# The last 256 tokens of a down projection, turned to have tokens on partitions

## The chip, the core and the metric

The kernel runs on one core of a Trainium2 chip. The core has five engines that run their own instruction streams and wait for each other by semaphores: TensorE (PE, matmuls; its weight loads are listed apart as PEld), VectorE (DVE), ScalarE (ACT), GpSimd (POOL) and SyncE (SP), which here issues most of the DMA transfers. SBUF is the memory on the core, with 128 partitions; PSUM is where matmuls accumulate, in eight banks of 512 fp32 columns. The metric is the device time of one execution in microseconds (us).

## The reference

One layer of an encoder: 2048 tokens, 1024 features. A first RMSNorm and projection, a state-space head group and an attention head group, an output projection; then the part that matters here:

```python
    x = x + mixed @ w_out[l]
    h2 = rmsnorm(x, norm_ffn_g[l])
    x = x + (jax.nn.silu(h2 @ w_gate[l]) * (h2 @ w_up[l])) @ w_down[l]
return rmsnorm(x, norm_final_g)
```

with `rmsnorm(x, g) = x * rsqrt(mean(x * x) + 1e-6) * g`, the mean over the 1024 features of a token. The inner width of the feed-forward part is 2816 = 22 x 128.

## The kernel before, in words

Through the whole kernel activations lie with features on partitions and tokens along the columns. Every matmul in the projections is computed from two fp32r parts of each operand (`split`: a high part by a cast on ACT, a low part by a subtraction on DVE), as three matmuls: high by high, high by low, low by high (`mm3`). fp32r is the reduced fp32 format that the large matmuls use; plain fp32 is used in the small ones: sums against a column of ones, and transposes against the identity.

The phases follow each other: first projection with the set-up of the state-space part (its xt tiles come from a pool of eight buffers), attention and state space, output projection, gate and up projection, down projection. Tile pools give buffers by turn; a scheduler sets the order of each engine's queue, except that PE's instructions keep the order of the program. `high_priority` moves a block ahead in the scheduler's order.

At the start of the gate and up phase SP issues the loads of `lo` (L1370), 20 transfers of 256 KB that bring the transformed activations. The output projection's last two blocks are still running then: they add to `xt` (L1148), store it to DRAM (L1149), square it on ACT (L1154) and load the next `xt` (L1140).

The down projection works in two halves of 1024 tokens. Eight tiles `acc0` to `acc7` (128 features by 1024 tokens each) start as the residual and collect the products. For the second half, 18 of the 22 inner tiles go through `group`; the last four go through `down`, in the token blocks of `TAIL`: 512, 256 and 256 tokens. Per block, `down` takes the eight feature tiles as 4, 2 and 2; per tile it runs 4 x 3 matmuls with the weights of the tile on the array and the block's tokens as moving columns, then DVE adds the bank to `acc` (L1582), and the block's `End` squares the result on ACT and adds up the squares on DVE (L1596 to L1600).

The final norm of a block needs the sum of squares over features, which here is over partitions. `sums` (L1602) multiplies the squares by a column of ones on PE, which gives one value per token, with tokens on partitions; `newton` (L98 to L111) makes the inverse root of it on DVE: 14 small instructions, five to set up and nine for three rounds. `products` (L1607) spreads the values over partitions again by transposes on PE (L79), copies them to SBUF on ACT (L141; the last block reads PSUM), multiplies each `acc` tile by gain and root on DVE (L1612), and stores it (L1613). The sums and products of a block are called between the tile groups of the next one; those of the last block have nothing behind them:

```python
        last.sums(True)
        last.products()
```

Of the kernel before, what the change touches and what calls it, by code (L numbers as in the profile page):

```python
# [16 lines left out]
P = 128  # L17
# [34 lines left out]
ORDER = "sptf"  # L52
PINA = True
X1B = 6
TAIL = (0, 512), (512, 256), (768, 256)
MAGIC = 12582912.0
F2 = NF // 2
SB_, CB_, GB_ = 5, 5, 10
# [52 lines left out]
    return o  # L111


def tok_sums(k, te, ps, c, sq):

    for i in range(4):
        te.matmul(ps[:, c + i : c + i + 1], sq[:, i * P : (i + 1) * P], k.ones[:], start=True, stop=True)


def spread(k, te, pb, o, c):  # L120
# [2 lines left out]
        te.transpose(pb[:, i * P : (i + 1) * P], o[:, c + i : c + i + 1].to_broadcast([P, P]), k.ident[:])  # L123


def rstd_steps(k, te, psum, pool, tag, sq, n, out, nt=None, **kw):

    nt = nt or out.shape[-1] // P
    ps = k.t(psum, *tag, **kw)
    sqs = sq if isinstance(sq, list) else [sq]  # L130
    for i in range(nt):
        for m, sq in enumerate(sqs):
            te.matmul(ps[:, i : i + 1], sq[:, i * P : (i + 1) * P], k.ones[:], start=m == 0, stop=m == len(sqs) - 1)
    with k.tc.high_priority():
        o = newton(k, pool, ps[:, :nt], n, nt)
    yield
    pb = k.t(psum, *tag, **kw)
    for i in range(nt):
        te.transpose(pb[:, i * P : (i + 1) * P], o[:, i : i + 1].to_broadcast([P, P]), k.ident[:])
    if out is not None:  # L140
        k.nc.scalar.copy(out, pb[:, : nt * P])  # L141
    yield pb
# [1371 lines left out]
def down_phase(k, S):  # L1514
    tc, nc, io = k.tc, k.nc, k.io
    V, te = nc.vector, k.te
    with ExitStack() as cx:
# [67 lines left out]
        class End:  # L1585
# [13 lines left out]
                    nc.scalar.activation(t[:, :n], self.acc[i][:, self.ts], AF.Square)  # L1599
                    nc.vector.tensor_tensor(self.sa[m][:, :n], self.sa[m][:, :n], t[:, :n], op=ALU.add)  # L1600

            def sums(self, last=False):  # L1602
                self.rs = None if last else k.t(fa, "rs", [P, 512])
                self.r = rstd_steps(k, k.te, dy, fa, ("ps", [P, 512]), self.sa, D, self.rs[:, : self.n] if self.rs else None, nt=self.n // P)
                next(self.r)

            def products(self):  # L1607
                pb = next(self.r)
                rs = self.rs or pb
                for i, a in enumerate(self.acc):  # L1610
                    v = a[:, self.ts]
                    nc.vector.scalar_tensor_tensor(v, v, k.go[:, i : i + 1], rs[:, : self.n], op0=ALU.mult, op1=ALU.mult)  # L1612
                    nc.sync.dma_start(io["out"][i * P : (i + 1) * P, self.out], a[:, self.ts])  # L1613

        ends = []
        for hf in range(2):
            acc = []
            f0 = 0
            for n, g in enumerate(DGROUPS[hf]):
                group(hf, f0, g, acc, (hf, n) == (0, 0))  # L1620
                f0 += g
                if n in (0, 1):
                    for e in ends:
                        (e.sums, e.products)[n]()
            if hf == 0:
                ends = [End(hf, acc, t, 512) for t in (0, 512)]
                for e in ends:
                    for i in range(KT):
                        e.square(i)
        hs, ds = zip(*((operand(S["h"][m : m + 1]), operand(S["wt"][m : m + 1])) for m in range(4)))  # L1630
        last = None
        for t0, tn in TAIL:
            e = End(1, acc, t0, tn)
            for n, i in enumerate((0, 4, 6)):
                down(hs, ds, range(i, (4, 6, 8)[n]), acc, t0, tn, e)
                if last and n < 2:
                    (last.sums, last.products)[n]()
            last = e
        last.sums(True)
        last.products()  # L1640


def block_kernel(tc, io, phases="pusamf"):
    nc = tc.nc
    k = K(tc, io)
    k.ssm_eng = nc.gpsimd
    with ExitStack() as cx:
        dram = cx.enter_context(tc.tile_pool(name="dram", bufs=1, space=bass.MemoryType.DRAM))
        cp = cx.enter_context(tc.tile_pool(name="const", bufs=1))
# [19 lines left out]
        k.ones = k.t(cp, "ones", [P, 1])  # L1669
        nc.vector.memset(k.ones[:], 1.0)  # L1670
# [12 lines left out]
        with tc.tile_pool(name="mf", reuse_waits="tile", bufs=1) as mf:  # L1683
            with pp() as psum, tc.tile_pool(name="mx", reuse_waits="tile", bufs=1) as mx:
                k.psum, k.mf, k.mx = psum, mf, mx
                for _ in mix:
                    pass
            gate_up_phase(k, S)
            down_phase(k, S)
    return k  # L1690


def layout(inputs):
# [15 lines left out]
    def cg(v):  # L1709
# [9 lines left out]
        "g_mix": cols(a["norm_mix_g"][0]), "g_ffn": cols(a["norm_ffn_g"][0]), "g_final": cols(a["norm_final_g"]),  # L1719
# [27 lines left out]
```

## Time and profile before

| what | us |
|---|---|
| median of 3 runs | 2242.87 (2241.45 to 2247.27) |
| profiled execution | 2241.38 |
| its span, first to last instruction | 2239.6 |
| PE busy in the span | 2153.6 (96%) |
| DVE busy | 1543.1 (69%) |
| ACT busy | 1004.6 (45%) |
| mean granted clock of TensorE | 0.988 |

The span is the part that the trace shows; the execution's own time lies 1.8 us above it. A row of a timeline gives start and duration in us, engine, line, operation, what is written and read, and in brackets how long the engine stood idle before it and what released it. The durations of matmuls contain their way through the array; the distance from start to start is what one costs in a row of them. In groups, the last columns are busy time in us, mean ns of one, and the idle time ahead with its releasers.

### The profile page before, as it was taken

What the parts mean: (1) busy time and instruction counts of PE and PEld (TensorE: products, weight loads), DVE (VectorE), ACT (ScalarE), POOL (GpSimd) and SP (SyncE); (2) the same over time, 40 slices, a digit from 0 to 9 for tenths busy, and PEclk for the clock granted to TensorE, in tenths of its full rate; (3) what the DMA queues carried; (4) which work ended last, traced back from release to release, by engine and by line L of the source; (5) the groups of instructions that cost most, each with busy time, mean ns of one, the idle gap of its engine ahead of it and who ended that gap; (6) DMA issues with size and microseconds to landing.
All of it is one profiled execution on the core that took longest, in us unless ns stands there. A gap on an engine that the chain in (4) does not pass through costs nothing.

```text
span 2239.6 us, 30165 instructions
## 1 busy us (share of the span) xinstructions
PE 2153.6 (96%) x10632; PEld 1819.1 (81%) x10632; DVE 1543.1 (69%) x2706; ACT 1004.6 (45%) x1667; POOL 354.1 (16%) x830
## 2 busy tenths in 40 slices
PE   8988898999988999999999999999999999999997
PEld 6777797999977788788888887888888788888886
DVE  8756767555557666767766768767665577688776
ACT  6355565556567541443333335333333343353322
POOL 3354666666600000000000000000000100000000
PEclk9999999999999999999999999999999999999999
DMA  9778867666552436835645557546333495465642
GB/s 330 231 249 283 270 207 229 193 196 193 179 175 99 137 116 206 275 118 173 198 153 200 198 191 258 199 160 207 108 115 97 136 371 198 159 226 183 217 174 76
DMA packets 194664, 430.16 MB, mean 192 GB/s; under 512 B 19792, under 2 KB 38272, under 8 KB 187408
## 3 DMA queue, kind: packets, MB, share of 16 engines
q1 hardware_dynamic: 186768, 403.26, 54.3%
q0 software_dynamic: 7744, 24.97, 3.6%
q8 instruction: 83, 1.36, 0.3%
q14 instruction: 69, 0.57, 0.1%
HBM read 288.95 MB, written 131.10 MB: 188 GB/s over the span
## 4 chain that ended last, share of the span: by engine, by line
PE 81%; DMA 7%; DVE 6%; ACT 2%; issue 2%; SPq 1%; DVEq 0%; ACTq 0%
PE X L76 20%; PE ps L76 18%; PE pf L76 11%; PE Y L76 10%; PE big L76 7%; PE W L76 5%; PE pj L76 4%; PE pt L79 2%; PE sc L76 2%; DMA acc<-x 1%; DMA hd<-wc 1%; DMA x<-xt 1%; DMA lo<-hc 1%; DMA w<-wss 1%; DVE ptl L900 0%
## 5 line engine op out<-in xcount | busy, mean ns | idle before, releaser
L76 PE MATMUL X<-hi,c 128*128 128x512 f32 x1408 | 450.9, 391 | 6.5 <-DVE c L153 3.4
L76 PE MATMUL ps<-hd,hd 128*128 128x512 f32 (+1 forms) x1968 | 428.1, 379 | 3.3 <-DVE hd L153 2.0
L76 PEld LDWEIGHTS ps<-hd,hd 128*128 128x128 f32 x1968 | 356.4, 188 | 73.6 <-DVE hd L153 2.7
L76 PEld LDWEIGHTS X<-hi,c 128*128 128x128 f32 x1408 | 264.9, 188 | 63.6 <-DVE c L153 4.5
L76 PE MATMUL X<-lo,c 128*128 128x512 f32 x704 | 274.7, 390 | 0.0
L153 ACT CAST hd<-hd 128x1536 fp32r<-128x1536 f32 (+1 forms) x106 | 147.5, 1394 | 231.0 <-DMA hd<-hq 174.6
L76 PE MATMUL Y<-hi,c 128*128 128x512 f32 x704 | 225.2, 390 | 2.4 <-DVE u L1428 2.4
L153 DVE TENSOR_TENSOR hd<-hd 128x1536 fp32r<-128x1536 f32 (+1 forms) x106 | 174.1, 1644 | 38.6 <-ACT hd L153 38.3
L1532 POOL DMA_DIRECT2D hd<-hq x7 | 5.3, 757 | 1165.3 <-PE X L76 1151.2
L153 DVE TENSOR_TENSOR c<-S,c 128x512 fp32r<-128x512 f32 x176 | 120.9, 688 | 99.3 <-ACT c L153 99.0
L1424 ACT COPY u<-X 128x512 f32<-128x512 f32 x132 | 77.5, 588 | 197.4 <-PE X L76 197.3
L153 ACT CAST c<-S 128x512 fp32r<-128x512 f32 x176 | 109.4, 622 | 120.8 <-PE Y L76 61.8
L76 PE MATMUL big<-m,woh 128*128 128x512 f32 x512 | 161.5, 397 | 0.0
L76 PEld LDWEIGHTS Y<-hi,c 128*128 128x128 f32 x704 | 132.6, 188 | 31.0 <-DVE u L1428 3.2
L1566 DVE TENSOR_TENSOR acc<-acc,ps 128x512 f32<-128x512 f32 x196 | 130.1, 682 | 37.9 <-PE ps L76 37.7
L76 PEld LDWEIGHTS X<-lo,c 128*128 128x128 f32 x704 | 132.7, 188 | 27.4
L153 ACT CAST c<-raw 128x512 fp32r<-128x512 f32 x132 | 82.2, 623 | 150.2 <-PE Y L76 73.0
L76 PE MATMUL pf<-hi,w 128*128 128x512 f32 x416 | 148.7, 409 | 0.0
L76 PE MATMUL Y<-lo,c 128*128 128x512 f32 x352 | 137.2, 390 | 0.0
L900 DVE TENSOR_TENSOR ptl<-pt,pth 128x640 fp32r<-128x640 f32 (+3 forms) x152 | 98.3, 647 | 54.6 <-ACT pth L899 53.1
L884 ACT ACTIVATE s<-s,mn 128x640 f32<-128x640 f32 (+4 forms) x128 | 97.9, 765 | 61.9 <-DVE mn L881 58.6
L899 ACT CAST pth<-pt 128x640 fp32r<-128x640 f32 (+3 forms) x152 | 83.7, 551 | 83.2 <-PE pt L79 78.8
(451 smaller groups left out, 4269.1 us busy)
## 6 DMA issues: line engine op xcount, KB each, us to landing
w<-wss SPq DMA_DIRECT2D x36, 1024.0 KB, 6.2
hq<-g SPq DMA_DIRECT2D x140, 256.0 KB, 2.1
hd<-hq SPq DMA_DIRECT2D x35, 768.0 KB, 4.4
hd<-wc SPq DMA_DIRECT2D x35, 768.0 KB, 5.8
raw<-in_w_gate SPq DMA_DIRECT2D x44, 512.0 KB, 3.7
raw<-in_w_up SPq DMA_DIRECT2D x44, 512.0 KB, 4.1
wc<-px SPq DMA_DIRECT2D x66, 256.0 KB, 3.1
wss<-w SPq DMA_DIRECT2D x12, 1024.0 KB, 6.1
```

The lines of the kernel that those rows point to most:

```text
L76: return self.tc.keep_in_program_order(self.tc.nc.tensor.matmul(*a, **b))
L79: return self.tc.keep_in_program_order(self.tc.nc.tensor.transpose(*a, **b))
L153: return nc.scalar.copy(hi, raw), nc.vector.tensor_tensor(lo, raw, f32(hi), op=ALU.subtract)
L884: nc.scalar.activation(s[:, :nk], s[:, :nk], AF.Exp, bias=mn[:], scale=-1.0, accum_out=sums[sb, pr][:, hh, qp : qp + 1])
L899: nc.scalar.copy(pth[:, a:b, qp, :], pt[:, a:b, :])
L900: nc.vector.tensor_tensor(ptl[:, a:b, qp, :], pt[:, a:b, :], f32(pth[:, a:b, qp, :]), op=ALU.subtract)
L1424: nc.scalar.copy(u[:], ps[:])
L1532: (nc.gpsimd if aside else nc.sync).dma_start(f32(lo), src.rearrange("g p c -> p g c"))
L1566: V.tensor_tensor(a, a, ps[:], op=ALU.add)
```

## The change

The `TAIL` keeps the blocks of 512 and of 256 tokens. The last 256 tokens are computed by a new function `by_tokens`, twice, for 128 tokens each, with the operands exchanged: the tokens' activations are the weights on the array, and 512 of the 1024 output features are the moving columns. The result has tokens on partitions. For each of two feature halves (c = 0, 1), 12 matmuls of 512 columns go into one bank, and after the first three of them four plain fp32 matmuls of the `acc` tiles against the identity, which add the residual, transposed, to the bank. The sum of squares is then along a row, and ACT squares and sums a bank in one instruction (`accum_out`). The mean, the root and the root's inverse are values per partition: ACT takes the square root, DVE a reciprocal, and one Newton round corrects it (`refine`). The first half's product with the gain is taken ahead and scaled on ACT; the second half's is one DVE instruction. A block is stored in two transfers of 128 tokens by 512 features, into an output of its own, `out_t`, that is joined to the other on the host.

Since gains now lie along a row, a new input `g_row` is loaded into all 128 partitions, into the tile `rsn`, whose first half is free after the output projection's part. `root`, with the same square root, reciprocal and one round, takes the place of `newton` for the blocks of 512 and 256 tokens of the second half. One square root is called ahead of the tail, so that the table of that function is loaded there.

The core of the diff:

```diff
-TAIL = (0, 512), (512, 256), (768, 256)
+TAIL = (0, 512), (512, 256)
+TOKENS = 768, 896
...
+def root(k, pool, ps, n, w):
+
+    V = k.nc.vector
+    v, f, y, o = (k.t(pool, t, [P, w], bufs=2) for t in ("nv", "nf", "ny", "no"))
+    k.nc.scalar.activation(o[:], ps, AF.Sqrt, scale=1.0 / n, bias=k.eps)
+    V.tensor_scalar(v[:], ps, -0.5 / n, -0.5 * EPS, op0=ALU.mult, op1=ALU.add)
+    return refine(V, v, f, y, o)
+
+def refine(V, v, f, y, o):
+
+    V.reciprocal(y[:], o[:])
+    V.tensor_tensor(f[:], y[:], y[:], op=ALU.mult)
+    V.tensor_tensor(f[:], f[:], v[:], op=ALU.mult)
+    V.scalar_tensor_tensor(o[:], f[:], 1.5, y[:], op0=ALU.add, op1=ALU.mult)
+    return o
...
+        def by_tokens(t0, hs, ds, acc):
+
+            ts = slice(t0, t0 + P)
+            m = (t0 // P) % 2
+            ps = [bank(dx) for _ in range(2)]
+            g, ta = S["rsn"][:, :D], S["rsn"][:, D + m * 512 : D + m * 512 + 512]
+            sq = [k.t(fa, f"q{c}", [P, 1], bufs=2) for c in range(2)]
+            v, f, y, o = (k.t(fa, n, [P, 1], bufs=2) for n in ("nv", "nf", "ny", "no"))
+            for c in range(2):
+                for n, ((hh, hl), (dh, dl)) in enumerate(zip(hs, ds)):
+                    mm3(te, ps[c][:], hh[:, 0, ts], hl[:, 0, ts], dh[:, 0, c * 512 : c * 512 + 512], dl[:, 0, c * 512 : c * 512 + 512], n == 0, n == len(hs) - 1, skip_group_check=True)
+                    if n == 0:
+                        for i in range(4):
+                            te.matmul(ps[c][:, i * P : (i + 1) * P], acc[4 * c + i][:, ts], k.ident[:], start=False, stop=False, skip_group_check=True)
+                    if n % 2:
+                        yield
+                j = k.t(fa, "sg", [P, 512], bufs=2)
+                with tc.high_priority():
+                    nc.scalar.activation(j[:], ps[c][:], AF.Square, accum_out=sq[c][:])
+                    if c == 0:
+                        V.tensor_tensor(ta, ps[0][:], g[:, :512], op=ALU.mult)
+                        V.tensor_scalar(f[:], sq[0][:], 1.0 / D, EPS, op0=ALU.mult, op1=ALU.add)
+                        V.tensor_scalar(y[:], f[:], -0.5, None, op0=ALU.mult)
+            b = k.t(fa, "ob", [P, 512])
+            with tc.high_priority():
+                nc.scalar.activation(o[:], sq[1][:], AF.Sqrt, scale=1.0 / D, bias=f[:])
+                V.tensor_scalar(v[:], sq[1][:], -0.5 / D, y[:], op0=ALU.mult, op1=ALU.add)
+                refine(V, v, f, y, o)
+                nc.scalar.activation(ta, ta, AF.Copy, scale=o[:])
+                V.scalar_tensor_tensor(b[:], ps[1][:], o[:], g[:, 512:], op0=ALU.mult, op1=ALU.mult)
+            rows = slice(t0 - TOKENS[0], t0 - TOKENS[0] + P)
+            nc.sync.dma_start(io["out_t"][rows, :512], ta)
+            nc.sync.dma_start(io["out_t"][rows, 512:], b[:])
+            yield
...
+        nc.sync.dma_start(S["rsn"][:, :D], bass.AP(io["g_row"].tensor, io["g_row"].offset, [[0, P], [1, D]]))
         hs, ds = zip(*((operand(S["h"][m : m + 1]), operand(S["wt"][m : m + 1])) for m in range(4)))
+        nc.scalar.activation(k.t(fa, "q0", [P, 1], bufs=2)[:], k.eps, AF.Sqrt)
         last = None
         for t0, tn in TAIL:
             e = End(1, acc, t0, tn)
             for n, i in enumerate((0, 4, 6)):
                 down(hs, ds, range(i, (4, 6, 8)[n]), acc, t0, tn, e)
-                if last and n < 2:
-                    (last.sums, last.products)[n]()
+                if last and n == 0:
+                    last.sums(root=root)
+                if last and n == 1:
+                    last.products()
             last = e
-        last.sums(True)
-        last.products()
+        for n, _ in enumerate(chain.from_iterable(by_tokens(t0, hs, ds, acc) for t0 in TOKENS)):
+            if n == 2:
+                last.sums(root=root)
+            if n == 5:
+                last.products()
```

What it does to the queues is seen in the order of the built programs. First PE at the very end. `hd` are the split operands, `ps` the PSUM banks, `sa` and `sb` sums of squares, `no` the inverse root. Before, the last two feature tiles of the last block, its sums and its transposes:

```order
L76 MATMUL ps_19990<-hd_19514,hd_19518 128x256 x3
L76 MATMUL ps_19989<-hd_19522,hd_19526 128x256 x3
L76 MATMUL ps_19990<-hd_19522,hd_19526 128x256 x3
L76 MATMUL ps_20023<-ones_85,sa_19898 128x1
L76 MATMUL ps_20023<-ones_85,sb_19901 128x1
...
L79 MATMUL ps_20046<-ident_80,no_20031 128x128 x2
```

Now, from the middle of the second token block's first half (the two transposes are those of the 256 block):

```order
L81 MATMUL ps_19933<-ident_80,no_19889 128x128 x2
L78 MATMUL ps_19915<-hd_19520,hd_19516 128x512 x3
L78 MATMUL ps_19915<-hd_19528,hd_19524 128x512 x3
L78 MATMUL ps_19916<-hd_19504,hd_19500 128x512 x3
L78 MATMUL ps_19916<-ident_80,acc_3276_18347 128x128
L78 MATMUL ps_19916<-ident_80,acc_3277_18348 128x128
L78 MATMUL ps_19916<-ident_80,acc_3278_18349 128x128
L78 MATMUL ps_19916<-ident_80,acc_3279_18350 128x128
L78 MATMUL ps_19916<-hd_19512,hd_19508 128x512 x3
L78 MATMUL ps_19916<-hd_19520,hd_19516 128x512 x3
L78 MATMUL ps_19916<-hd_19528,hd_19524 128x512 x3
```

Nothing of PE is left behind the last projection matmul; the sums and transposes of the 256 block have moved between the matmuls of the token blocks.

Then DVE at the end. Before, the last block's additions and its Newton root, of which the first rows stand here (eight more and eight products follow):

```order
L1582 TENSOR_TENSOR acc_3278_18348<-acc_3278_18348,ps_19989 128x256
L1582 TENSOR_TENSOR acc_3279_18349<-acc_3279_18349,ps_19990 128x256
L1600 TENSOR_TENSOR sb_19901<-sb_19901,sg_20016 128x256
L1600 TENSOR_TENSOR sa_19898<-sa_19898,sg_20020 128x256
L102 TENSOR_SCALAR nv_20028<-ps_20023 128x2
L103 CAST nf_20029<-nv_20028 128x2
L104 TENSOR_SCALAR nf_20029<-nf_20029 128x2
L106 TENSOR_SCALAR nv_20028<-nv_20028 128x2
L105 CAST ny_20030<-nf_20029 128x2
L108 TENSOR_TENSOR nf_20029<-ny_20030 128x2
```

Now, all that follows the fifth product of the 256 block (`q` are the sums of squares of a half, `ob` the second half's result):

```order
L1655 TENSOR_TENSOR rsn_92<-ps_19915,rsn_92 128x512
L1656 TENSOR_SCALAR nf_19920<-q_3435_19917 128x1
L1632 SCALAR_TENSOR_TENSOR acc_3277_18348<-acc_3277_18348,g_final_90,rs_19880 128x256
L1657 TENSOR_SCALAR ny_19921<-nf_19920 128x1
L1632 SCALAR_TENSOR_TENSOR acc_3278_18349<-acc_3278_18349,g_final_90,rs_19880 128x256
L1632 SCALAR_TENSOR_TENSOR acc_3279_18350<-acc_3279_18350,g_final_90,rs_19880 128x256
L1661 TENSOR_SCALAR nv_19919<-q_3436_19918,ny_19921 128x1
L127 RECIPROCAL ny_19921<-no_19922 128x1
L128 TENSOR_TENSOR nf_19920<-ny_19921 128x1
L129 TENSOR_TENSOR nf_19920<-nf_19920,nv_19919 128x1
L130 SCALAR_TENSOR_TENSOR no_19922<-nf_19920,ny_19921 128x1
L1664 SCALAR_TENSOR_TENSOR ob_19982<-ps_19916,no_19922,rsn_92 128x512
```

Behind the last square DVE now has four small steps and one product in place of the root's fourteen and eight products.

Last, SP's queue at the start of the gate and up phase, far from the code's place of the new load. Before, stores of `hc` end and the loads of `lo` begin:

```order
L1323 DMA hc_72<-gh_2036_9941 128x512
L1149 DMA x_5_67<-xt_9846 128x2x512
L1323 DMA hc_72<-gh_2038_9945 128x512
L1323 DMA hc_72<-gl_2037_9943 128x512
L1370 DMA lo_2044_10043<-hc_72 128x512
L1370 DMA lo_2050_10085<-hc_72 128x512
```

Now:

```order
L1343 DMA hc_72<-gh_2036_9942 128x512
L1169 DMA x_5_67<-xt_9847 128x2x512
L1343 DMA hc_72<-gh_2038_9946 128x512
L1343 DMA hc_72<-gl_2037_9944 128x512
L1685 DMA rsn_92<-in_g_row 128x1024
L1390 DMA lo_2044_10044<-hc_72 128x512
L1390 DMA lo_2050_10086<-hc_72 128x512
```

The load of the gains has gone in ahead of the first of the 20 loads; the rows behind it are the same, one place later.

More of the change, by code (lines that the diff above doesn't have):

```diff
@@ L111, in newton @@
     return o
+def root(k, pool, ps, n, w):
[10 more added lines that the diff above has]
+    return o
 def tok_sums(k, te, ps, c, sq):
     for i in range(4):
-        te.matmul(ps[:, c + i : c + i + 1], sq[:, i * P : (i + 1) * P], k.ones[:], start=True, stop=True)
+        te.matmul(ps[:, c + i : c + i + 1], sq[:, i * P : (i + 1) * P], k.ones, start=True, stop=True)
 def spread(k, te, pb, o, c):
@@ L123, in spread, with rstd_steps @@
         te.transpose(pb[:, i * P : (i + 1) * P], o[:, c + i : c + i + 1].to_broadcast([P, P]), k.ident[:])
-def rstd_steps(k, te, psum, pool, tag, sq, n, out, nt=None, **kw):
+def rstd_steps(k, te, psum, pool, tag, sq, n, out, nt=None, root=newton, **kw):
     nt = nt or out.shape[-1] // P
@@ L132, in rstd_steps @@
         for m, sq in enumerate(sqs):
-            te.matmul(ps[:, i : i + 1], sq[:, i * P : (i + 1) * P], k.ones[:], start=m == 0, stop=m == len(sqs) - 1)
+            te.matmul(ps[:, i : i + 1], sq[:, i * P : (i + 1) * P], k.ones, start=m == 0, stop=m == len(sqs) - 1)
     with k.tc.high_priority():
-        o = newton(k, pool, ps[:, :nt], n, nt)
+        o = root(k, pool, ps[:, :nt], n, nt)
     yield
@@ L1600, in square, with sums @@
                     nc.vector.tensor_tensor(self.sa[m][:, :n], self.sa[m][:, :n], t[:, :n], op=ALU.add)
-            def sums(self, last=False):
-                self.rs = None if last else k.t(fa, "rs", [P, 512])
-                self.r = rstd_steps(k, k.te, dy, fa, ("ps", [P, 512]), self.sa, D, self.rs[:, : self.n] if self.rs else None, nt=self.n // P)
+            def sums(self, **kw):
+                self.rs = k.t(fa, "rs", [P, 512])
+                self.r = rstd_steps(k, k.te, dy, fa, ("ps", [P, 512]), self.sa, D, self.rs[:, : self.n], nt=self.n // P, **kw)
                 next(self.r)
             def products(self):
-                pb = next(self.r)
-                rs = self.rs or pb
+                next(self.r)
+                rs = self.rs
                 for i, a in enumerate(self.acc):
@@ L1668, in block_kernel @@
         k.ident = ident
-        k.ones = k.t(cp, "ones", [P, 1])
-        nc.vector.memset(k.ones[:], 1.0)
+        one = k.t(cp, "ones", [P, 2])
+        k.ones, k.eps = one[:, :1], one[:, 1:]
+        nc.vector.memset(k.ones, 1.0)
+        nc.vector.memset(k.eps, EPS)
         k.gm, k.gf, k.go = (k.t(cp, n, [P, KT]) for n in ("g_mix", "g_ffn", "g_final"))
@@ L1741 @@
         io[name] = nc.dram_tensor(f"in_{name}", a.shape, mybir.dt.from_np(a.dtype), kind="ExternalInput").ap()
-    io["out"] = nc.dram_tensor("out", (D, SEQ), F32, kind="ExternalOutput").ap()
+    io["out"] = nc.dram_tensor("out", (D, TOK), F32, kind="ExternalOutput").ap()
+    io["out_t"] = nc.dram_tensor("out_t", (SEQ - TOK, D), F32, kind="ExternalOutput").ap()
     with tile.TileContext(nc) as tc:
@@ L1745 @@
     r = run_bass_kernel_spmd(nc, [arrays], core_ids=[0])
-    return np.ascontiguousarray(r.results[0]["out"].T)[None]
+    return np.ascontiguousarray(np.concatenate([r.results[0]["out"].T, r.results[0]["out_t"]]))[None]
```

3 lines of the change are left out of this document (2 added, 1 removed).

## The prediction

> **What bounds the kernel now.** First the page: its span, and the chain of work that ended last, by engine.
>
> ```profile
> span 2239.6 us, 30165 instructions
> PE 81%; DMA 7%; DVE 6%; ACT 2%; issue 2%; SPq 1%; DVEq 0%; ACTq 0%
> ```
>
> TensorE (PE) is the bound for most of the span, so a change is worth what it takes from the places where PE is not the last to end. The table by stretches, asked around the end of the program (busy us of PE, PEld, DVE, ACT, POOL, then clock and DMA), shows such a place.
>
> ```profile
> 2200.00:2220.00 20.00, 18.79 (x159) 18.58 (x158) 15.18 (x50) 5.22 (x13) 0.00 (x0) 1.00 0.28 106
> 2220.00:2230.00 10.00, 4.99 (x40) 4.50 (x38) 7.74 (x30) 1.94 (x5) 0.00 (x0) 1.00 0.30 106
> 2230.00:2240.00 10.00, 0.66 (x2) 0.29 (x2) 4.45 (x16) 0.00 (x0) 0.00 (x0) 0.50 0.30 106
> ```
>
> In the last 20 us PE works for less than 6. The timeline of PE there (start, duration, what, and in brackets the idle time before and who ended it), then of DVE, and the output line:
>
> ```profile
> 2203.26 3.11 PE L76 MATMUL ps<-hd,hd 128*128 128x256 f32 x24
> 2207.59 0.65 PE L79 MATMUL ps<-ident,no 128*128 128x128 f32 x4 [1.21 <-DVE no L110]
> 2207.99 8.88 PE L76 MATMUL ps<-hd,hd 128*128 128x256 f32 x72
> 2216.71 0.28 PE L76 MATMUL ps<-ones,sa 128*128 128x1 f32 x2
> ...
> 2222.03 0.43 PE L79 MATMUL ps<-ident,no 128*128 128x128 f32 x2 [1.40 <-DVE no L110]
> 2222.21 3.12 PE L76 MATMUL ps<-hd,hd 128*128 128x256 f32 x24
> 2227.85 0.38 PE L76 MATMUL ps<-ones,sa 128*128 128x1 f32 x2 [2.52 <-DVE sa L1600]
> ...
> 2231.62 0.66 PE L79 MATMUL ps<-ident,no 128*128 128x128 f32 x2 [2.72 <-DVE no L110]
> ```
>
> ```profile
> 2232.32 3.22 DVE L1612 SCALAR_TENSOR_TENSOR acc<-acc,g_final,ps 128x256 f32<-128x256 f32 x8 [0.85 <-PE ps L79]
> ```
>
> ```profile
> L1613 SPq DMA_DIRECT2D out<-acc x24: 332/364/537, 2209.7 to 2236.6; - x24
> ```
>
> The last projection matmul ends at 2222.21 + 3.12 = 2225.33; the span runs 14.27 us more. In it a chain passes from engine to engine: additions and squares (to 2227.85), sums over features, the Newton root (2.72 of waiting), the transposes, eight products, stores. The last store is issued at 2236.6 and the span ends 3.0 later.
>
> **The change, part by part: prices.** The change keeps everything up to the first 256-token block, and replaces the second (96 matmuls of 256 columns) by two blocks of 128 tokens with 24 matmuls of 512 columns each, plus 16 matmuls against the identity that bring in the residual. The rows for each kind, PE first:
>
> ```profile
> 2149.77 30.54 PE L76 MATMUL ps<-hd,hd 128*128 128x512 f32 x134
> ```
>
> ```profile
> 2202.45 0.95 PE L76 MATMUL ps<-ones,sa 128*128 128x1 f32 x8
> ```
>
> ```profile
> 337.18 0.59 PE L76 MATMUL pj<-rsn,Tm 128*128 128x256 f32 x2
> 337.61 0.59 PE L76 MATMUL pj<-XG,Vm 128*128 128x256 f32 x2
> ```
>
> A 256-column matmul costs (2216.71 - 2207.99) / 72 = 0.121, a 512-column one 30.54 / 134 = 0.228. An identity matmul is in plain fp32 with 128 columns, which no row has. In fp32 each instruction makes two records: L76 pj, with 256 columns, takes 0.43 (337.18 to 337.61). Half of that is 0.215, if the columns set the pace; 0.43 is the upper bound, if they don't. As the lower one, the eight records with one column (four instructions, 2202.45 to 2203.26) give 0.20, for the weight loads alone. I take 0.23, near the column rate: 16 x 0.23 = 3.7 (3.2 to 6.9).
>
> Then ACT and DVE, as groups, steps and lines:
>
> ```profile
> L1599 ACT ACTIVATE sg<-acc 128x256 f32<-128x256 f32 x12 | 4.7, 415 | 14.8 <-DVE acc L1582 9.6 <-DVE nf L108 4.4 <-DVE nf L103 0.8
> L1612 DVE SCALAR_TENSOR_TENSOR acc<-acc,g_final,rs 128x512 f32<-128x512 f32 x8 | 5.4, 745 | 1.0 <-ACT rs L141 1.0
> L1599 ACT ACTIVATE sg<-acc 128x512 f32<-128x512 f32 x7 | 4.4, 633 | 8.6 <-DVE acc L1582 7.7 <-DVE sa L1600 0.7
> ```
>
> ```profile
> L443 ACT ACTIVATE hi<-xt,g_mix 128x512 fp32r<-128x512 f32 x16 | 11.0, 722 | 7.0 <-DMA xt<-in_xp 6.3 <-DVE nf L108 0.4 <-DVE ny L110 0.3
> L452 ACT ACTIVATION_READ_ACCUMULATOR w<-w 128x1 f32 x16 | 2.9, 184 | 0.0
> ```
>
> ```profile
> 2229.75 0.16 DVE L108 TENSOR_TENSOR nf<-ny 128x2 f32<-128x2 f32 x1
> 2229.94 0.16 DVE L109 TENSOR_TENSOR nf<-nf,nv 128x2 f32<-128x2 f32 x1
> ```
>
> ```profile
> L262 DVE RECIPROCAL small<-small x1: 246/246/246, 16.6 to 16.6; 128x16 f32<-128x16 f32 x1
> ```
>
> A square with its accumulator read: 0.63 + 0.18 = 0.81. A square root of a few columns, of which the trace has none: the two squares give 0.415 - (0.633 - 0.415) = 0.20 at width zero, and a per-partition operand adds 0.09 (722 against 633), so 0.30, between the 0.18 of the accumulator read and the 0.42 of 256 columns. A small step on DVE 0.19 from start to start; a reciprocal 0.25. A product of 512 columns 0.745, of 256 columns 3.22 / 8 = 0.40.
>
> **The projection, on PE.** From 2203.26: 24 x 0.121 = 2.90, to 2206.16. The 1.21 wait before the transposes goes: the root now is one ACT instruction and five on DVE in place of fourteen. The sums end at 2202.45 + 0.95 = 2203.40; 0.3 on ACT, then 0.16 + 0.25 + 3 x 0.19 on DVE and two additions of 256 columns between them, 0.4 each, put the result at about 2205.5, before PE asks for it. If it were late, PE would wait at most the old 1.21. Four transposes 0.40 (2207.59 to 2207.99); 24 more 2.90, to 2209.46; 48 x 0.228 = 10.94; identities 3.7; the sums of the 256 block 0.81, its two transposes 0.18 (2222.03 to 2222.21); 0.16 for the last one's end. Sum: 2225.25, against 2225.33. PE gains nothing: what it saves in waits and columns it spends on identities, and on the sums and transposes that have moved between the matmuls.
>
> These sums wait for the 256 block's squares, which stand on DVE behind the products of the 512 block:
>
> ```profile
> 2208.89 5.39 DVE L1612 SCALAR_TENSOR_TENSOR acc<-acc,g_final,rs 128x512 f32<-128x512 f32 x8 [1.02 <-ACT rs L141]
> ```
>
> They start some 1.3 earlier now, at 2207.6, and take 5.4, with one addition of 0.4 between them, to 2213.4; the last two tiles' additions and squares, 0.4 each in turn, take 1.6 more: 2215.0. PE comes to the sums at 2209.46 + 18 x 0.228 + 8 x 0.23 = 2215.4. This cover is thin: a delay of DVE beyond 0.4 shows on PE. The old last block's additions, squares and sums of squares (eight, eight and six) fall away, so nothing else crowds the two queues.
>
> **The end behind the last matmul.** In a row: square 0.81, root 0.30, reciprocal and three steps 0.25 + 0.58 = 0.83, the product of 512 columns 0.75, with ACT's scaling of the other half (0.72) beside it. Then SP: the first store 0.37, the second issued, and 3.0 from there as now. Hand-overs 0.2. Sum 6.26 in place of 14.27: the end comes at 2231.5, or 8.1 earlier. Half a us more or less, as the second store has 256 KB where the last one had 128.
>
> What else stands on DVE there: five products of the 256 block, the product of the first half, three more products. They end at about 2225.3, the last square at 2226.1, so 0.8 covers them; each us beyond shows at the end.
>
> **What it adds elsewhere.** The load of the gains over all partitions (512 KB) stands on SP's queue where the order shows it: ahead of the 20 loads of lo at the start of the gate and up phase.
>
> ```profile
> 916.00:920.00 4.00, 4.00 (x20) 3.30 (x19) 4.00 (x8) 3.63 (x7) 0.00 (x0) 1.00 1.04 383
> ```
>
> ```profile
> 907.65 12.95 SPq L1370 DMA_DIRECT2D lo<-hc  x20
> 920.93 0.37 SPq L1149 DMA_DIRECT2D x<-xt  x1
> 929.40 0.90 SPq L1140 DMA_DIRECT2D xt<-in_xt  x2
> ```
>
> ```profile
> 933.62 2.47 DVE L1148 TENSOR_TENSOR xt<-xt,big 128x1024 f32<-128x1024 f32 x2 [4.29 <-DMA xt<-in_xt]
> 936.23 0.64 PE L76 MATMUL X<-hi,c 128*128 128x512 f32 x1 [1.84 <-DVE xt L1148]
> ```
>
> ```profile
> SPq L1140 <- DMA x<-xt: 5.4, 1, 5.4
> ```
>
> The DMA engines are full there (share 1.04), and the queue issues 256 KB per 12.95 / 20 = 0.65, so 512 KB are 1.3. Behind those loads waits the store of x, for its landing wait (5.4) a square and the next load of xt, for that DVE, and for DVE PE, already idle for 1.84. No step has slack, so PE idles 1.3 more. Bounds: 0, should the start of the loads have been waiting for something else, and 2.6 if a repeated source costs double. I take 1.3.
> The Trainium skill, "DMA: Bandwidth & Descriptors", section "Rules for kernel authors", says that a zero-stride broadcast of c copies as the outermost dimension confines a DMA to at most c engines if c is below 16. Here c is 128, so by that rule the price stays 1.3; no row of this trace shows such a broadcast.
>
> The table of the square root is loaded between the last cast and the copy of u:
>
> ```profile
> 1774.54 0.59 ACT L1424 COPY u<-X 128x512 f32<-128x512 f32 x1 [1.67 <-PE X L76]
> ```
>
> ```profile
> 671.68 1.28 ACT L884 ACT_TABLE_LOAD   x1
> ```
>
> 1.28 + 0.20 fits into the 1.67 of idle time, so nothing; at most some 0.3 if it didn't.
>
> **The sum.** -8.1 + 1.3 = -6.8, against this execution's own 2241.38 us (its span and 1.8 around it). The median of the runs shown, 2242.87, is 1.5 above that; from it the forecast is 2236.1. The bound of what a measurement of this kernel can tell from no change, 0.3% or 6.7 us, is 2236.1 as well: the forecast stands on the edge.
>
> **The rivals.** (1) The gain load is hidden: 1.3 comes back, 2234.8. For it: the row at 907.65 follows other waits on that queue. Against: the full DMA engines. (2) Identity matmuls at the upper price, or DVE late at the sums: PE ends up to 3.2 later, 2239.3. For it: four identities stand in a row and each loads other weights; against: the one-column row, where the loads alone take 0.20. (3) Slower: the gain load runs through few engines or reads its one row at a crawl. Through one engine it takes 16 x 1.3 = 21, all of it on the chain through x to PE: 20 more, 2256. It decides from 1.3 + 6.8 + 6.7 = 14.8 on. Against: 128 rows go to 128 partitions as in other loads of 512 KB.
>
> **How the numbers follow.** Forecast 0.52, spread 2234.5 to 2238 by the small terms and the runs' own spread, half of it beyond the bound; rival 1 0.20, nearly all faster; rival 2 0.20, within; rival 3 0.06; 0.02 for other delays. Faster 0.26 + 0.19 + 0.03 = 0.48 with the share of noise, slower 0.06, the same 0.46. The range runs from rival 1 less the half us of the stores and a us of spread, 2233.2, to rival 2 with another 1.5 of spread, 2240.8.
>
> **What would show it.** Right: in the profile after, PE's last matmul near 2226.5 (the 1.3 included), the span's end 6 to 6.5 behind it, no wait ahead of the first transposes, PE's idle time at the first X matmul near 3.1, identity records about 0.115 apart. Wrong: a wait of PE at the sums, squares that end after DVE's products, a chain behind the last matmul above 8, or a stall of SP behind the gain load.

## The result, and the profile after

The changed kernel takes 2239.36 us (median; 2233.12 to 2244.18) against 2247.27 us for the kernel before in the same session (2241.45 to 2250.46). The ratio is 0.9964, with a 95% interval from 0.9956 to 0.9973: by it 8.1 us less, between 6.1 and 9.9 (the two medians lie 7.9 apart). A second session gave 0.9965 (0.9953 to 0.9978). The bound of 0.3% lies inside both intervals.

The profiled execution of after has a span of 2238.5 us, against 2239.6 of before. The two spans differ by only 1.1 us, because PE came late to the end in this execution, by 6.5 us; the section on the hardware has what the traces show of that. So the end is read from a point inside the program: from the column sums of the 512-token block to the end of the span. Before, that is 2202.45 to 2239.6, or 37.15 us. After, in the timeline (start, duration, engine, line, what; in brackets the idle time before and who ended it):

```profile
2208.97 0.95 PE L78 MATMUL ps<-ones,sa 128*128 128x1 f32 x8
...
2212.74 0.60 PE L81 MATMUL ps<-ident,no 128*128 128x128 f32 x4
...
2216.74 1.05 PE L78 MATMUL ps<-ident,acc 128*128 128x128 f32 x8
...
2217.55 3.02 PE L78 MATMUL ps<-hd,hd 128*128 128x512 f32 x12
...
2220.97 0.42 DVE L1620 TENSOR_TENSOR sa<-sa,sg 128x256 f32<-128x256 f32 x1
...
2221.99 0.28 PE L78 MATMUL ps<-ones,sa 128*128 128x1 f32 x2
...
2229.68 2.32 PE L78 MATMUL ps<-hd,hd 128*128 128x512 f32 x9
...
2232.03 0.60 ACT L1653 ACTIVATE sg<-ps 128x512 f32<-128x512 f32 x1 [2.97 <-PE ps L78]
...
2233.92 0.75 DVE L1664 SCALAR_TENSOR_TENSOR ob<-ps,no,rsn 128x512 f32<-128x512 f32 x1
2234.61 0.33 SPq L1666 DMA_DIRECT2D out_t<-rsn  x1
2235.05 0.37 SPq L1667 DMA_DIRECT2D out_t<-ob  x1
```

From 2208.97 to 2238.5 it is 29.53 us: 7.62 less. The transposes at 2212.74 have no wait ahead of them (1.21 before). PE's last product ends at 2229.68 + 2.32 = 2232.00, and the span's end lies 6.50 behind it, where it was 14.27. From the sums to PE's last product it is 23.03 now and was 22.88: as forecast, the whole gain lies behind the last product.

The second place is the load of the gains. In the same profile SP issues it, and PE begins the first X product:

```profile
907.69 1.21 SPq L1685 DMA_DIRECT2D rsn<-in_g_row  x1
...
938.14 0.47 PE L78 MATMUL X<-hi,c 128*128 128x512 f32 x1 [1.78 <-DVE xt L1168]
```

The load takes SP 1.21 us ahead of the lo loads, and the X product starts 30.45 us behind its issue; before, it started 28.58 behind the issue of the first lo load. PE's idle time there is 1.78, no more than the 1.84 of before, so this profile alone could mean that the load is hidden. The runs below were made to tell.

### The profile page after: what moved, and what is told of

Same layout as the page of the kernel before. It is cut to its first block, busy times and chain, and to the rows that moved or that the text cites. A ratio compares the mean times of both kernels' runs of the same rounds, so it can differ in the third digit from the quotient of the medians.

```text
span 2238.5 us, 30079 instructions
## 1 busy us (share of the span) xinstructions
PE 2162.0 (97%) x10606; PEld 1823.2 (81%) x10606; DVE 1536.4 (69%) x2671; ACT 1008.3 (45%) x1675; POOL 353.5 (16%) x830
## 4 chain that ended last, share of the span: by engine, by line
PE 83%; DMA 6%; DVE 6%; issue 3%; ACT 2%; SPq 0%; POOL 0%; DVEq 0%; ACTq 0%; POOLq 0%
PE X L78 21%; PE ps L78 18%; PE Y L78 11%; PE pf L78 10%; PE big L78 9%; PE W L78 5%; PE pj L78 4%; PE pt L81 2%; PE sc L78 2%; DMA hs<-g 1%; DMA acc<-x 1%; DVE ptl L920 0%; DMA xt<-in_xt 0%; DMA xt<-in_xp 0%; DVE s L901 0%
```

## The experiments

**The load of the gains, put later.** A one-column copy on DVE makes it wait until the first half of the down projection is done; the rest is the kernel after.

```diff
                 for e in ends:
                     for i in range(KT):
                         e.square(i)
+                V.tensor_copy(S["rsn"][:, :1], acc[KT - 1][:, HALF - 1 :])
+                nc.sync.dma_start(S["rsn"][:, :D], bass.AP(io["g_row"].tensor, io["g_row"].offset, [[0, P], [1, D]]))
...
-        nc.sync.dma_start(S["rsn"][:, :D], bass.AP(io["g_row"].tensor, io["g_row"].offset, [[0, P], [1, D]]))
```

> The kernel after with the load of the gains (512 KB) taken from its place ahead of the lo loads and put into the middle of the down projection. Theory of the forecast, the load costs 1.3 us on the chain from the lo loads over the store of x to the first X product: 1.3 us faster than the kernel after, some 9.4 faster than the kernel before (ratio 0.9958); in the trace the store of x is issued 1.4 earlier, at about 921, and PE reaches the first X product 1.3 earlier than with the load where the clock is the same. Rival 1, the load is hidden: the same time as the kernel after (0.9964). Nothing else changes, the tail behind PE's last product stays at 6.5.

Measured: 2236.62 us against 2244.48 of before, ratio 0.9967 (0.9955 to 0.9979). The trace (SP's and PE's timeline):

```profile
907.65 12.94 SPq L1390 DMA_DIRECT2D lo<-hc  x20
...
936.04 0.47 PE L78 MATMUL X<-hi,c 128*128 128x512 f32 x1 [1.78 <-DVE xt L1168]
```

The chain is 2.1 shorter than in the first profile of after (28.39 against 30.45). The time does not show it: 0.9967 against 0.9964, with intervals of 2.5 us to each side.

**The kernel after once more**, for a second profile.

> The kernel after once more, beside the runs that follow, and with a second profile. Where the profile of after differs from that of before by the clock alone, this profile shows other half-clock stretches than the first, and PE comes to the sums of the 512 block at another time; the stretch from there to the end is 28.7 again. The store of x behind the lo loads is issued at about 922.4 and the first X product starts 30.4 behind the issue of the gain load, as in the first profile, if the chain and not PE sets it. Ratio to before 0.9964.

Measured: 2238.56 against 2245.89, ratio 0.9965 (0.9953 to 0.9978). The same rows:

```profile
904.93 0.56 SPq L1685 DMA_DIRECT2D rsn<-in_g_row  x1
...
934.98 0.47 PE L78 MATMUL X<-hi,c 128*128 128x512 f32 x1 [3.15 <-DVE xt L1168]
...
2202.64 0.95 PE L78 MATMUL ps<-ones,sa 128*128 128x1 f32 x8
```

The chain takes 30.05 and PE idles 3.15, the 3.1 that the forecast named. In the first profile PE itself was about 2 us late there, and so met the late chain with the old idle time. The stretch from the sums to the end is 29.56 (2202.64 to 2232.2).

**Transfers that nothing needs, ahead of the lo loads.** The load of the gains is late, and at its old place the tile is written to memory: twice in two transfers, or four times in one.

```diff
+        V.memset(S["rsn"][:, :1], 0.0)
+        for m in range(2):
+            nc.sync.dma_start(S["gx"][m], S["rsn"][:, :D])
```

> The load of the gains is in the middle of the down projection (as in the run with the late load), and at its old place ahead of the 20 lo loads SP issues two transfers of 512 KB that nothing needs (the tile that the gains go to, written to memory), twice the bytes of the load. Theory of the forecast, each 512 KB ahead of the lo loads costs 1.3 us on the path: 2.6 slower than with the late load (ratio to before 0.9970), and the first X product of PE 2.6 later against its neighbours. Rival 1, such transfers are hidden there: the same as the late load.

```diff
+        V.memset(S["rsn"][:, :1], 0.0)
+        nc.sync.dma_start(S["gx"], S["rsn"][:, :D].rearrange("p (n d) -> p n d", n=1).to_broadcast([P, 4, D]))
```

> As the late load, with one transfer of 2 MB that nothing needs (four times the tile of the gains to memory) ahead of the 20 lo loads, four times the bytes of the gain load. By the forecast's price (1.3 us per 512 KB on the path): 5.2 slower than with the late load, ratio to before 0.9990. By the price that the last two traces give (2.1 to 2.4 us per 512 KB from the first issue to the first X product): 8.4 to 9.4 slower, ratio 1.0005 to 1.0009. If such transfers are hidden: 0.9967 as with the late load.

Measured: 1 MB 2240.57 us, ratio 0.9984 (0.9971 to 0.9997); 2 MB 2242.10 us, ratio 0.9986 (0.9973 to 0.9999). Against the two kernels with the late load (0.9967 here, 0.9964 further below; mean 0.99655) these are 4.2 and 4.6 us, each uncertain by some 3.5. The forecast's price (2.6 and 5.2) lies within that; the dearer one of the second expectation (8.4 to 9.4) does not. The traces, of the 1 MB run and then of the 2 MB run:

```profile
916.25 2.02 SPq L1672 DMA_DIRECT2D gx<-rsn  x2
...
949.36 0.77 PE L78 MATMUL X<-hi,c 128*128 128x512 f32 x1 [4.67 <-DVE xt L1168]
```

```profile
911.19 0.61 SPq L1671 DMA_DIRECT2D gx<-rsn  x1
...
946.12 0.77 PE L78 MATMUL X<-hi,c 128*128 128x512 f32 x1 [8.09 <-DVE xt L1168]
```

From SP's first issue at this place to the first X product, over all profiles (some of them of runs that follow below):

| at this place | us from SP's first issue to the first X product |
|---|---|
| nothing | 28.6, 28.4 (before); 28.9 (before with the root alone); 28.4, 29.5, 29.4 (late load) |
| the load of the gains, 512 KB | 30.5, 30.1 (after); 30.3 (after with the layout alone); 29.9, 30.0 (after without the residual, after with half a store) |
| 1 MB written | 33.1 |
| 2 MB written | 34.9 |

The means of the first two rows are 28.9 and 30.1, and the two rows do not overlap: the load costs this chain 1.3 us. The two written amounts cost 4.2 and 6.1, or 2.1 and 1.5 per 512 KB; around them the scheduler also set a few instructions of ACT and DVE in another order, so these prices are less clean. That the additions at this place are all hidden is excluded for 2 MB: its 4.6 us, in which the other order has its part, stand clear of their uncertainty. How much of the 1.3 of the single load reaches the end is left open, since the times of the early and the late load differ by 0.2 us with an uncertainty of 2.5.

**The root alone.** The kernel before, with ACT's square root in place of the Newton steps in the end's three blocks.

```diff
-        o = newton(k, pool, ps[:, :nt], n, nt)
+        o = root(k, pool, ps[:, :nt], n, nt)
...
-                    (last.sums, last.products)[n]()
+                    last.products() if n else last.sums(root=root)
...
-        last.sums(True)
+        last.sums(True, root=root)
```

> The kernel before with the square root of ACT in place of the Newton steps in the three blocks at the end, and nothing else of the change. If the root gives what the trace of before suggests: the waits of PE ahead of the two groups of transposes (1.21 and 1.40) go, and the last root takes 1.1 in place of 2.5, so 4.0 us less than before (ratio 0.9982), about half of the change. Rival, the layout does all of it, since the waits only move to the squares and products on DVE: under 1.5 us less (0.9993 or above).

Measured: 2241.58 against 2244.48, ratio 0.9990 (0.9977 to 1.0003), too wide to decide. The trace does (PE's rows):

```profile
2206.54 0.95 PE L76 MATMUL ps<-ones,sa 128*128 128x1 f32 x8
...
2210.30 0.60 PE L79 MATMUL ps<-ident,no 128*128 128x128 f32 x4
...
2223.13 0.38 PE L79 MATMUL ps<-ident,no 128*128 128x128 f32 x2
...
2229.55 0.38 PE L76 MATMUL ps<-ones,sa 128*128 128x1 f32 x2 [3.16 <-DVE sa L1618]
...
2231.90 0.66 PE L79 MATMUL ps<-ident,no 128*128 128x128 f32 x2 [1.30 <-DVE no L128]
```

Both waits ahead of the first two groups of transposes are gone and the last is 1.30 in place of 2.72. A part of the gain comes back at the last block's sums, where PE waits 3.16 for DVE in place of 2.52. From the sums to the end it is 33.36 (2206.54 to 2239.9), 3.8 less than before. The rival (the layout does it all) falls.

**The layout alone.** The kernel after with the Newton steps everywhere, written for one column in the blocks by tokens.

```diff
-                last.sums(root=root)
+                last.sums()
...
-                nc.scalar.activation(o[:], sq[1][:], AF.Sqrt, scale=1.0 / D, bias=f[:])
-                V.tensor_scalar(v[:], sq[1][:], -0.5 / D, y[:], op0=ALU.mult, op1=ALU.add)
-                refine(V, v, f, y, o)
+                V.tensor_scalar(v[:], sq[1][:], 1.0 / D, f[:], op0=ALU.mult, op1=ALU.add)
+                iterate(V, v, f, y, o)
```

> The kernel after with the Newton steps in place of the root everywhere (and without the table load of the root). The wait ahead of the first transposes comes back (1.2), and the root of the last block takes 2.7 in place of 1.1: 2.8 us slower than the kernel after, some 5.2 faster than before (ratio 0.9977). If the layout does all of it: as the kernel after (0.9964). If the root does all of it: as the kernel before (1.000).

Measured: 2242.39 against 2244.48, ratio 0.9988 (0.9977 to 0.9999). From the sums to the end it is 32.60 (2202.90 to 2235.5): 4.55 less than before and 3.07 more than after, with the old wait back:

```profile
2202.90 0.95 PE L78 MATMUL ps<-ones,sa 128*128 128x1 f32 x8
...
2208.04 0.65 PE L81 MATMUL ps<-ident,no 128*128 128x128 f32 x4 [1.21 <-DVE no L117]
```

The two parts give 3.8 and 4.55 alone and 7.62 together. The 0.7 that they share fits the second group of transposes, which waited 1.40 before and does not wait in either kernel: with the root alone, the 0.64 that PE waits longer at the last sums leaves 0.76 of that.

**The residual left out.** The kernel after without the 16 products against the identity.

```diff
-                    if n == 0:
-                        for i in range(4):
-                            te.matmul(ps[c][:, i * P : (i + 1) * P], acc[4 * c + i][:, ts], k.ident[:], start=False, stop=False, skip_group_check=True)
```

> The kernel after without the 16 products against the identity, so the residual (and what the earlier groups gave) is left out for the last 256 tokens. They take 16 x 0.20 = 3.2 us of PE. If PE alone sets the time there, the stretch from the sums of the 512 block to the end is 3.2 shorter (25.5 in place of 28.7, ratio 0.9950). If the additions and squares on DVE are late for the sums of the 256 block once the eight identities ahead of them are gone (cover 0.5 to 0.6 in the trace, 1.6 taken away): a wait of 1.0 there, and 2.2 shorter (26.5, ratio 0.9954). If the identities were hidden: no change.

Measured: 2237.91 against 2245.89, ratio 0.9967 (0.9954 to 0.9979). The trace:

```profile
2205.41 0.95 PE L78 MATMUL ps<-ones,sa 128*128 128x1 f32 x8
...
2217.88 0.38 PE L78 MATMUL ps<-ones,sa 128*128 128x1 f32 x2 [1.13 <-DVE sa L1620]
```

From the sums to the end it is 27.29 (to 2232.7), 2.24 less than after. The wait of 1.13 at the sums of the 256 block is the thin cover of DVE that the forecast spoke of, now gone. The products cost 2.24 + 1.13 = 3.4 us of PE. The time, which should have fallen by 2, did not show it.

**The last store on another queue.** With the late load; only the very last store is issued by ACT.

```diff
-            nc.sync.dma_start(io["out_t"][rows, 512:], b[:])
+            (nc.scalar if m else nc.sync).dma_start(io["out_t"][rows, 512:], b[:])
```

> The late load of the gains, and the very last store, of the second half of the last block, issued by ACT in place of SP, so that it doesn't stand behind the store of the first half. In the trace the last product ends 0.4 ahead of the last issue: the end should come 0.35 earlier behind PE's last product (6.1 in place of 6.5). In the time no more than that: ratio 0.9955 if the late load gives 2, 0.9963 if it gives nothing.

Measured: 2237.35 against 2245.89, ratio 0.9964 (0.9952 to 0.9977). The trace:

```profile
2203.86 0.95 PE L78 MATMUL ps<-ones,sa 128*128 128x1 f32 x8
...
2229.49 0.33 SPq L1666 DMA_DIRECT2D out_t<-rsn  x1
2229.58 0.38 ACTq L1667 DMA_DIRECT2D out_t<-ob  x1
```

The issue comes 0.09 behind the first one instead of 0.44, and the end (2233.4) comes no earlier: from the sums it is 29.54, as in the other kernels (29.53, 29.56, 29.49). The expected 0.35 is missing. In all four the end lies 3.9 behind the issue of the first of the two stores.

**One of the two last stores left out** (2244.18 us, timed once).

```diff
-            nc.sync.dma_start(io["out_t"][rows, :512], ta)
+            if not m:
+                nc.sync.dma_start(io["out_t"][rows, :512], ta)
```

> The kernel after without the store of the first half (256 KB) of the very last block, whose output is left out. In the traces so far the end lies 3.9 us behind the issue of the first of the last two stores, whether the second one is issued 0.44 (SP) or 0.09 (ACT) behind it. If the 512 KB of both together set the end: the one store that is left is issued some 0.1 behind its product and the end comes 3.0 to 3.2 behind its issue, so PE's last product to the end falls from 6.5 to about 5.7. If each store's own landing sets it (3.45 behind its issue as now): about 6.1.

```profile
2234.03 2.32 PE L78 MATMUL ps<-hd,hd 128*128 128x512 f32 x9
...
2239.04 0.33 SPq L1668 DMA_DIRECT2D out_t<-ob  x1
```

The end (2242.4) comes 3.36 behind this issue and 6.05 behind PE's last product. So the sizes of the first theory (3.0 to 3.2, 5.7) fall, and those of the second (3.45, about 6.1) come close: on SP's queue the second store ended nearly as fast as one does alone. The pair ends 3.9 behind its first issue, one store 3.36: the second 256 KB add about 0.5, and issuing them earlier than SP does gained nothing. The DMA engines' share (the column ahead of the last one) says why, here of the first profile of after:

```profile
2235.60:2236.60 1.00, 0.00 (x0) 0.00 (x0) 0.00 (x0) 0.00 (x0) 0.00 (x0) 1.00 1.07 414
2236.90:2238.50 1.60, 0.00 (x0) 0.00 (x0) 0.00 (x0) 0.00 (x0) 0.00 (x0) 0.50 0.00 0
```

and of the run on two queues:

```profile
2230.50:2231.50 1.00, 0.00 (x0) 0.00 (x0) 0.00 (x0) 0.00 (x0) 0.00 (x0) 0.57 1.04 404
2231.80:2233.40 1.60, 0.00 (x0) 0.00 (x0) 0.00 (x0) 0.00 (x0) 0.00 (x0) 0.50 0.00 0
```

In both the engines are full (1.07 and 1.04) from 1.0 to 2.0 us behind the first issue, they move nothing from 2.3 behind it on, and the span ends 1.6 later. With two stores on two queues the full engines set the end, so that the earlier issue had nothing to gain. The Trainium skill, "DMA: Bandwidth & Descriptors", section "Issuing engines are not separate DMA queues", says that transfers from several engines interleave on the same DMA engines, so that a second issuer saves no more than issue time; the 0.35 that did not come agrees.

**The refinement left out.** With the late load, the blocks by tokens use the reciprocal of the root without the Newton step behind it.

```diff
-                V.tensor_scalar(v[:], sq[1][:], -0.5 / D, y[:], op0=ALU.mult, op1=ALU.add)
-                refine(V, v, f, y, o)
-                nc.scalar.activation(ta, ta, AF.Copy, scale=o[:])
+                V.reciprocal(y[:], o[:])
+                nc.scalar.activation(ta, ta, AF.Copy, scale=y[:])
```

> The late load of the gains, and in the two blocks with tokens on partitions the reciprocal of the square root as it is, without the Newton step behind it (three small steps on DVE and what prepares them). The three steps take 0.6 between the last square and the last products, so the end comes 0.6 earlier behind PE's last product: 5.9 in place of 6.5, and 28.9 in place of 29.5 from the sums of the 512 block to the end. In the time at most that (ratio 0.996). If something else were late there (the products of the 256 block on DVE), less than 0.6.

Measured: 2236.81 against 2246.11, ratio 0.9960 (0.9946 to 0.9974). The trace:

```profile
2209.82 0.95 PE L78 MATMUL ps<-ones,sa 128*128 128x1 f32 x8
...
2230.52 2.32 PE L78 MATMUL ps<-hd,hd 128*128 128x512 f32 x9
```

From the sums (2209.82) to the end (2238.8) it is 28.98, and behind PE's last product (2230.52 + 2.32) 5.96: 0.55 less, of the 0.6 that was expected. It is the fastest ratio of all, but its interval covers that of after.

**The kernel before once more** (2246.31 us, timed once).

> The kernel before once more with a profile. From the sums of the 512 block to the end it takes 37.1 again, PE idles 1.8 or more ahead of the first X product, and the chain from the start of the lo loads to that product takes 28.4 to 29.5, whatever half-clock stretches this execution has; where PE comes to those sums differs by these stretches.

```profile
908.76 12.80 SPq L1370 DMA_DIRECT2D lo<-hc  x20
...
937.11 0.47 PE L76 MATMUL X<-hi,c 128*128 128x512 f32 x1 [2.15 <-DVE xt L1148]
...
2207.37 0.95 PE L76 MATMUL ps<-ones,sa 128*128 128x1 f32 x8
```

The stretch from the sums to the end is 37.13 (2207.37 to 2244.5), the chain to the first X product 28.35, PE's idle time there 2.15. The span is 4.9 longer than in the first profile of before, and all of it lies ahead of the sums.

## Why the prediction was right, point by point

- **Direction and size.** The forecast was 6.8 us less; measured are 8.1 (6.1 to 9.9) by the ratio. 2239.36 lies in the stated range, 3.3 above the 2236.1. That gap is not the change's: the three times of before that the forecast started from had a median of 2242.87, the longer series 2247.27. Shifted by these 4.4, the range still holds the measured time. But 8.1 less is just what rival 1 (the load hidden) gives, so the time alone does not tell the forecast from this rival. (By its own sum the range begins at 2233.3, not at 2233.2.)
- **The end behind the last product: 6.26 forecast, 6.50 measured.** The single steps were a little cheaper (from PE's end to the first store's issue 2.61); of the five small steps that DVE has behind the last square one runs beside ACT's root, so four of them count. The term that was mis-sized is the last store: 3.0 behind its issue was carried over from a store of 128 KB, and the pair of 256 KB ends 3.45 behind the second issue. The half us for it was named beside the sum.
- **The projection on PE: unchanged, as forecast.** From the first product behind the sums of the 512 block to the last one it takes 22.21 (2209.79 to 2232.00), against 21.99 worked out and 22.07 before. A group of four identity products takes 0.81 (2216.74 to 2217.55) plus some 0.1 ahead of it, so 0.23 each; with all of them away PE saved 3.4, forecast 3.7. The pace of their records is 0.10, not the 0.115 that was named. That PE's last product would end near 2226.5 could not serve as a sign: it ended at 2232.00 in the first profile of after and at 2225.66 in the second.
- **The thin covers held.** DVE's last addition for the sums ended at 2221.39 and PE came at 2221.99 (0.6, forecast 0.4). That this cover is thin was shown by taking the identities away: a wait of 1.13.
- **The gain load: 1.3 forecast, 1.3 measured on the chain**, but not shown in the time. The sign that was named for it (idle time near 3.1) is missing in the first profile of after (1.78), where PE was late itself, and stands in two others (3.15, and 3.08 in the run with half a store). It tells little, though: with the load in its early place two more profiles have 2.79, and without it the idle time goes from 1.78 to 2.84. The reading rests on the chain's length. The measured terms sum to -7.6 + 1.3 = -6.3; the time says -8.1. The difference lies within the interval, and whether it is noise, or the wait for the load covers other waits in most executions, is open. Rival 1 fits the time better than the forecast does; against it stand the chain and the 2 MB run.
- **The root's table load: nothing.** In the trace of after it takes 1.28 and the root of the constant 0.20, and 0.43 of ACT's idle time is still left ahead of the copy of u:

```profile
1774.58 1.28 ACT L1687 ACT_TABLE_LOAD   x1
1775.88 0.20 ACT L1687 ACTIVATE q<-ones 128x1 f32<-128x1 f32 x1
1776.51 0.59 ACT L1444 COPY u<-X 128x512 f32<-128x512 f32 x1 [0.43 <-PE X L78]
```

- **Rivals 2 and 3 did not come.** DVE was not late at the sums, and the gain load landed 5.4 us behind its issue in the first profile of after and 5.0 in the second, not 21. The rule on zero-stride broadcasts that the forecast took from the Trainium skill ("DMA: Bandwidth & Descriptors", "Rules for kernel authors"), by which 128 copies outermost do not confine the transfer to few engines, agrees with these landings.

## What to carry to other kernels

The end of a kernel, behind the last matmul, is a chain without cover: there a reshaping that leaves PE's work as it is can pay by its whole shortening, and its steps can be summed from single rows to within half a us. When the effect is a few us in two thousand, compare profiles from a point inside the program, not by their spans; here the spans said 1.1, the stretch 7.6 and the ratio of the times 8.1. A load that "fits anywhere" made a chain 1.3 us longer here because it stood on a queue ahead of loads that this chain waits for; that the time grew by it was not shown. Such a price is read from the chain's length over several profiles, since PE's own idle time depends on when PE happens to arrive.

## What the runs showed of the hardware

The spans of one kernel differ by 5 to 6 us between executions (2239.6 and 2244.5 for before, 2238.5 and 2232.2 for after). One part of that is TensorE's granted clock, which drops to one half in stretches of 3.4 us or multiples of it, whose number and place change. Three of them in the first profile of after (columns: us, then busy us and count of PE, PEld, DVE, ACT, POOL, then the granted clock, the DMA engines' share, GB/s):

```profile
806.70:810.10 3.40, 3.40 (x10) 2.65 (x9) 3.40 (x19) 1.67 (x2) 0.00 (x0) 0.50 0.65 228
868.20:871.60 3.40, 3.40 (x10) 2.66 (x9) 3.40 (x18) 1.06 (x1) 0.00 (x0) 0.51 0.65 242
1851.20:1858.00 6.80, 5.84 (x14) 4.61 (x15) 6.54 (x8) 2.94 (x2) 0.00 (x0) 0.50 0.56 214
```

and the same places in the profile of before:

```profile
806.70:810.10 3.40, 3.40 (x19) 2.87 (x19) 3.03 (x19) 1.68 (x2) 0.00 (x0) 1.00 0.67 251
...
1851.20:1858.00 6.80, 6.80 (x31) 5.63 (x30) 6.80 (x7) 2.98 (x2) 0.00 (x0) 1.00 0.26 98
```

Each stretch of 3.4 us at half clock costs up to 1.7 us of PE's work: 10 products in place of 19 at the first place. Summed over the trace's clock records ahead of the sums, such stretches make 44.4 us in the profile of before and to 58.0 in that of after; half of the 13.6 between them is 6.8, about the 6.5 by which PE came late to the sums. Other pairs agree less well. The second profiles have 51.2 (before) and 47.8 (after): half of the differences is 3.4 of the 4.9 between the two of before, and 5.1 of the 6.3 between the two of after. The run with the layout alone has 58.0 as well, but its PE came to the sums at 2202.90, 0.5 behind the first profile of before where the clock would make 6.8. So the half clock is a part of what differs between executions, and the rest is open.

The Trainium skill, "TensorE: Matmul & The Clock Gate", section "What's actually happening", has a clock that goes to half after an idle window of some 3.4 us and windows that run freely. The third stretch comes near to that: in the 3.4 us ahead of it PE was busy for only 1.32.

```profile
803.30:806.70 3.40, 3.15 (x25) 2.89 (x24) 2.35 (x6) 1.22 (x2) 0.00 (x0) 1.00 0.19 70
864.80:868.20 3.40, 3.15 (x23) 2.84 (x23) 2.93 (x11) 0.59 (x1) 0.00 (x0) 0.99 0.41 154
...
1847.80:1851.20 3.40, 1.32 (x6) 0.75 (x4) 3.40 (x4) 1.49 (x1) 0.00 (x0) 1.00 0.23 40
```

The other two do not fit: PE was busy for 3.15 of the 3.4 us ahead of each, and the next stretch was at half clock all the same. In the profile of before PE was busy for the same 3.15 there, and the stretch behind it kept the full clock:

```profile
803.30:806.70 3.40, 3.15 (x24) 2.78 (x22) 2.01 (x3) 1.22 (x2) 0.00 (x0) 1.00 0.02 7
```

What starts these stretches stays open.
